# Decays and learning rates per 512 tokens, as short tiles beside the projection tiles

## The chip, the cores and the metric

The kernel runs on one core of one Trainium2 chip. The metric is the time of one execution on the device, in microseconds (us). Times are given as the median of several executions. The profile and the rows below come from one execution that the hardware profiler recorded.

## What is computed

The reference is one layer of a decoder trunk over 2048 tokens of 1024 features, in float32. A mixer sub-layer normalises the input, projects it (`h @ w_in`, 3344 columns) and hands the columns to two groups of heads: gated linear attention (GLA) and an RWKV-7 group, whose outputs go through `w_out`. A gated MLP with a causal convolution follows, the channel mixer. The change touches one part of the RWKV-7 group, where `p` is the token-shifted projection and `c0 : c1 : c2` bound two slices of 64 columns:

```python
w_log = -softplus(-(w0 + tanh(p[..., c0:c1]) @ w_up)) - 0.5
decay = exp(-exp(w_log))                        # per token and channel, 512 channels
a = sigmoid(a0 + p[..., c1:c2] @ a_up)          # the learning rate, 512 channels
k = k * (1 + (a - 1) * k_a)
```

So for each token two small products, each with 64 inputs and 512 outputs, give the logarithm of the decay, the learning rate `a`, and the factor by which `k` is multiplied.

## The kernel before

The 2048 tokens are cut into 4 blocks of 512. Features lie on the 128 partitions, tokens along the free dimension. For each block `stage_b` runs the input projection, one tile of 128 columns after the other: `gemm3` makes 24 matmuls of 128x512 into one PSUM bank (`gbank`, a ring of two banks), three for each of 8 parts of the input, because weight and activation are each split into a high and a low float32r part and three of the four products are kept. `evacuate` then reads the bank: for the RWKV tiles ScalarE scales it (L335), VectorE adds the shifted token (L336), GpSimd mends the first column (L337) and ScalarE keeps the last column for the next block (L338); the result goes to a DRAM tile (`pd`, L339). `ev`, the buffer of the result, is a ring of three.

Weights of the projection are loaded by `Weights`: in block 0 a part is loaded, cast by ScalarE (L190), its low part made by VectorE or GpSimd (L193), and both parts are stored to DRAM as `kept` (L200). Later blocks load the kept parts (L179) into the same two rings of six (`whi`, `wlo`); a projection tile takes two buffers of each.

The recurrences run on units of 128 tokens, 16 in all, 4 per block. `rwkv_p` prepares a unit: it loads its slice of the projections (L776 to L780), turns the values, and makes the decays and rates. That last part is what the change takes out: the tile `wa` holds 64 rows for the decay and 64 for the rate; ScalarE takes the tanh of the first (L792), TensorE makes 4 matmuls for each (L797, L798, plain float32, 64 rows of contraction, 128 tokens) into two banks `rp`, ScalarE takes a tanh of each quarter (L800, L803), GpSimd scales and shifts the results (L801, L805), and VectorE makes the factor of `k` (L804). Then a scan sums the logarithms of the decay (L808), and the rest of the unit follows.

The generator `stage_b` of the next block is the filler of the units: `fill()` is called at several places of a unit and takes, on average, 0.85 tiles each. Block 0's projections run before the units start, beside the first GLA chunks. While the last block's units run, the filler is `spare`, the output projection of the blocks already done. Nothing of the order on the engines is written out by hand: a planner orders all instructions by their priority and by a simulated timeline, gives each tile a free buffer of its ring, and places the waits. All loads are issued from SyncE's queue (SP), stores from SP or from ScalarE's queue.

The channel mixer runs after the units, with its own pools; the change does not touch it.

Of the kernel before, what the change touches and what calls it, by code (L numbers as in the profile page):

```python
# [9 lines left out]
F32 = mybir.dt.float32  # L10
F32R = mybir.dt.float32r
BF16 = mybir.dt.bfloat16
U32 = mybir.dt.uint32
AF = mybir.ActivationFunctionType
ALU = mybir.AluOpType

P = 128
D = 1024
KT = 8
NB = 512  # L20
# [75 lines left out]
def hybrid_kernel(ctx, tc, x, cst, vec, c_row, ada_t, w_in, w_v, w_first, w_z, gk_up, wa_up, g_up,  # L96
# [31 lines left out]
    def vcol(name, k=0, n=1):  # L128
        o, w = _VL[name]
        return vt[:, o + k:o + k + n]  # L130
# [8 lines left out]
    groups = ((TQ, 2), (TK, 2), (TV, 4), (TG, 4), (TZ, 1), (TR, 4), (TRK, 4), (TRV, 4), (TWA, 1), (TPG, 1))  # L139
    pd = [{t0: dram.tile([P, n, NB], F32, name=f"proj_{b}_{t0}") for t0, n in groups} for b in range(NBLK)]  # L140
    mixd = [dram.tile([P, 8, NB], F32, name=f"mix_{b}") for b in range(NBLK)]
# [185 lines left out]

    def evacuate(b, t, ps):
        ev = ap.tile([P, NB], F32, name="ev", tag="ev", bufs=pools["nev"])
        if t < TZ:  # L330
            A.activation(out=ev, in_=ps, func=AF.Copy, scale=0.125 if t < TK else 1.0)
        else:

            m = t - TR
            A.activation(out=ev, in_=ps, func=AF.Copy, scale=omu[:, m:m + 1])  # L335
            V.scalar_tensor_tensor(out=ev[:, 1:NB], in0=ps[:, 0:NB - 1], scalar=vcol("mu", m), in1=ev[:, 1:NB], op0=ALU.mult, op1=ALU.add)  # L336
            G.tensor_tensor(out=ev[:, 0:1], in0=ev[:, 0:1], in1=carry[:, m:m + 1], op=ALU.add)  # L337
            A.activation(out=carry[:, m:m + 1], in_=ps[:, NB - 1:NB], func=AF.Copy, scale=vcol("mu", m))  # L338
        (A if t < TZ else nc.sync).dma_start(out=dst_of(b, t), in_=ev)  # L339
# [23 lines left out]
    def stage_b(b):  # L363

        h = ahead.pop(b)[1]
        order = ([TZ] + list(range(8, TZ)) if b == 0 else list(range(8)) + [TZ] + list(range(8, TZ))) + [TWA, TPG] + [TR + i for i in range(12)]
        for i_, t in enumerate(order):
# [40 lines left out]
            evacuate(b, t, ps)  # L408
# [184 lines left out]
    wa_up = cst1([P, 512], "wa_up", wa_up)  # L593
# [13 lines left out]
    kah = cst1([P, 8], "kah")  # L607
# [162 lines left out]
    def rwkv_p(b, q, n):  # L770
# [3 lines left out]
        wa = ctile([P, CQ], F32, name="rw_wa", tag="rw_wa", bufs=1)  # L774
        pg = ctile([P, CQ], F32, name="rw_pg", tag="rw_pg", bufs=2)
        nc.sync.dma_start(out=wa, in_=pd[b][TWA][:, 0, cs])  # L776
# [15 lines left out]
        A.activation(out=wa[0:64], in_=wa[0:64], func=AF.Tanh)  # L792
        psw, psa = bank("rp"), bank("rp")
        pw_ = psw.rearrange("p (j t) -> p j t", j=4)
        pv = psa.rearrange("p (j t) -> p j t", j=4)
        for j in range(4):
            PE.matmul(out=pw_[:, j, :], lhsT=wa_up[0:64, j * P:(j + 1) * P], rhs=wa[0:64, :], start=True, stop=True)  # L797
            PE.matmul(out=pv[:, j, :], lhsT=wa_up[64:128, j * P:(j + 1) * P], rhs=wa[64:128, :], start=True, stop=True)  # L798
        for j in range(4):
            A.activation(out=lw[:, j], in_=pw_[:, j], func=AF.Tanh, scale=0.5, bias=w0h[:, j:j + 1])  # L800
        G.tensor_scalar(out=lw, in0=lw, scalar1=-0.5 * DECAY, scalar2=-0.5 * DECAY, op0=ALU.mult, op1=ALU.add)  # L801
        for j in range(4):
            A.activation(out=an[:, j], in_=pv[:, j], func=AF.Tanh, scale=0.5, bias=a0h[:, j:j + 1])  # L803
            V.tensor_scalar(out=kp_[:, j], in0=an[:, j], scalar1=kah[:, j:j + 1], scalar2=kah[:, 4 + j:5 + j], op0=ALU.mult, op1=ALU.add)  # L804
        G.tensor_scalar(out=an, in0=an, scalar1=-0.5, scalar2=-0.5, op0=ALU.mult, op1=ALU.add)  # L805
# [695 lines left out]
def layout(inputs):  # L1501
# [26 lines left out]
    for n in ("w0", "a0", "k_k", "k_a", "gn_g", "gn_b"):  # L1528
# [22 lines left out]
        "wa_up": np.concatenate([f("w_lora_up")[0], f("a_lora_up")[0]], 0),  # L1551
# [19 lines left out]
```

## Time and profile before

| | us |
|---|---|
| median of 3 executions | 2924.12 |
| lowest, highest | 2917.79, 2926.74 |
| the profiled execution, its own time | 2920.91 |
| its span (first to last instruction) | 2918.8 |
| TensorE busy in the span | 2746.2 (94%) |
| VectorE busy | 2080.9 (71%) |
| ScalarE busy | 1303.1 (45%) |
| GpSimd busy | 1083.5 (37%) |
| mean granted clock of TensorE | 0.963 |

In the rows below PE is TensorE's matmuls, PEld its weight loads, DVE is VectorE, ACT ScalarE, POOL GpSimd and SP SyncE; a q behind the name is the engine's queue, which issues DMAs. L797 is line 797 of the kernel. `A<-B,C` names the tile written and the tiles read, without buffer numbers. Matmuls overlap: the time from one start to the next is what one takes from the engine, and its own duration is longer. A float32 matmul is recorded as two.

### The profile page before, as it was taken

The numbers are of one execution on the slowest core, as the hardware profiler recorded it, in microseconds if no ns is written. First come the engines' busy times: TensorE is split into PE (matmuls) and PEld (weight loads), VectorE is DVE, ScalarE is ACT, GpSimd is POOL, SyncE is SP. The second block draws the span as 40 slices with busy tenths as digits, with TensorE's granted clock in tenths as the row PEclk, the third lists the DMA queues.
The fourth block names the chain that finished last, engine by engine and source line by source line (L and its number), as shares of the span: only waits on it lengthen the run. The fifth ranks groups of instructions, "written<-read, shape, count | busy, mean of one in ns | idle before, by whom it ended". The sixth has DMA issues, their size and how long they took to land.

```text
span 2918.8 us, 54644 instructions
## 1 busy us (share of the span) xinstructions
PE 2746.2 (94%) x20296; PEld 2224.0 (76%) x20296; DVE 2080.9 (71%) x4103; ACT 1303.1 (45%) x2721; POOL 1083.5 (37%) x1150
## 2 busy tenths in 40 slices
PE   6989999999999999899679999999997999999998
PEld 5777877877787777777567888888776788888887
DVE  7356877757766668876687595775868786685867
ACT  4454435445544455453344352443534444353443
POOL 5223212312122223332456354453436454363541
PEclk9999989999999998999889999999998999999999
DMA  8988955545555565655314424334564633425243
GB/s 285 342 292 305 311 159 175 162 138 164 177 165 145 167 192 189 185 164 168 122 54 152 156 76 159 101 117 149 183 225 140 215 94 128 141 87 162 90 130 110
DMA packets 363530, 486.90 MB, mean 167 GB/s; under 512 B 80768, under 2 KB 153728, under 8 KB 363264
## 3 DMA queue, kind: packets, MB, share of 16 engines
q1 hardware_dynamic: 327984, 447.75, 48.3%
q10 hardware_dynamic: 35280, 35.66, 3.6%
q8 instruction: 160, 2.62, 0.4%
q14 instruction: 106, 0.87, 0.1%
HBM read 342.77 MB, written 140.51 MB: 166 GB/s over the span
## 4 chain that ended last, share of the span: by engine, by line
PE 58%; DVE 10%; DMA 6%; issue 2%; ACT 2%; POOL 2%; SPq 0%; DVEq 0%; ACTq 0%; POOLq 0%
PE g_bank L1270 9%; PE g_bank L1268 9%; PE g_bank L1269 9%; PE g_bank L1325 5%; PE g_bank L1327 5%; PE g_bank L1326 5%; PE g_bank L281 3%; PE g_bank L282 3%; PE g_bank L283 3%; DVE rw_pr L901 1%; DMA rw_k<-proj 1%; DMA acc<-acc 1%; PE gl_bank L698 1%; DMA rw_ln<-inv_a 1%; POOL w_lo L1144 1%
## 5 line engine op out<-in xcount | busy, mean ns | idle before, releaser
L1268 PE MATMUL g_bank<-h_hi,w_hi 128*128 128x512 f32 x1232 | 486.9, 396 | 28.1 <-ACT h_hi L1143 17.2
L1269 PE MATMUL g_bank<-h_lo,w_hi 128*128 128x512 f32 x1232 | 485.8, 394 | 7.7 <-DVE h_lo L1144 4.3
L1270 PE MATMUL g_bank<-h_hi,w_lo 128*128 128x512 f32 x1232 | 478.9, 394 | 7.1 <-POOL w_lo L1144 7.0
L1143 ACT CAST w_hi<-w_st 128x512 fp32r<-128x512 f32 (+1 forms) x396 | 239.0, 608 | 487.0 <-PE g_bank L1326 336.6
L1328 DVE SCALAR_TENSOR_TENSOR acc<-g_bank,mod,acc 128x512 f32<-128x512 f32 (+1 forms) x200 | 144.8, 728 | 248.4 <-PE g_bank L1327 231.7
L281 PE MATMUL g_bank<-h_hi,w_hi 128*128 128x512 f32 x736 | 298.4, 406 | 7.6 <-DMA w_hi<-khi 5.7
L1144 POOL TENSOR_TENSOR w_lo<-w_st,w_hi 128x512 fp32r<-128x512 f32 x154 | 216.7, 1407 | 236.8 <-ACT w_hi L1143 226.0
L1268 PEld LDWEIGHTS g_bank<-h_hi,w_hi 128*128 128x128 f32 x1232 | 234.8, 191 | 82.4 <-ACT h_hi L1143 20.0
L282 PE MATMUL g_bank<-h_lo,w_hi 128*128 128x512 f32 x736 | 293.4, 399 | 0.0
L283 PE MATMUL g_bank<-h_hi,w_lo 128*128 128x512 f32 x736 | 293.3, 399 | 0.1
L1270 PEld LDWEIGHTS g_bank<-h_hi,w_lo 128*128 128x128 f32 x1232 | 234.0, 190 | 61.0 <-POOL w_lo L1144 12.4
L1269 PEld LDWEIGHTS g_bank<-h_lo,w_hi 128*128 128x128 f32 x1232 | 234.2, 190 | 58.8 <-DVE h_lo L1144 5.4
L1325 PE MATMUL g_bank<-hh,w_hi 128*128 128x512 f32 x640 | 251.1, 395 | 5.9 <-DVE acc L1328 5.8
L1326 PE MATMUL g_bank<-hl,w_hi 128*128 128x512 f32 x640 | 251.2, 395 | 0.0
L1327 PE MATMUL g_bank<-hh,w_lo 128*128 128x512 f32 x640 | 251.1, 394 | 0.0
L1144 DVE TENSOR_TENSOR w_lo<-w_st,w_hi 128x512 fp32r<-128x512 f32 (+1 forms) x242 | 201.4, 832 | 18.0 <-ACT w_hi L1143 12.3
L281 PEld LDWEIGHTS g_bank<-h_hi,w_hi 128*128 128x128 f32 x736 | 139.5, 190 | 41.4 <-DMA w_hi<-khi 3.0
L283 PEld LDWEIGHTS g_bank<-h_hi,w_lo 128*128 128x128 f32 x736 | 139.3, 189 | 30.7 <-DMA w_lo<-klo 0.8
L282 PEld LDWEIGHTS g_bank<-h_lo,w_hi 128*128 128x128 f32 x736 | 139.8, 190 | 27.4
L1325 PEld LDWEIGHTS g_bank<-hh,w_hi 128*128 128x128 f32 x640 | 119.8, 187 | 37.0 <-DVE acc L1328 7.1
L1327 PEld LDWEIGHTS g_bank<-hh,w_lo 128*128 128x128 f32 x640 | 119.8, 187 | 29.6
L1326 PEld LDWEIGHTS g_bank<-hl,w_hi 128*128 128x128 f32 x640 | 119.7, 187 | 29.1
(341 smaller groups left out, 6103.4 us busy)
## 6 DMA issues: line engine op xcount, KB each, us to landing
acc<-acc SPq DMA_DIRECT2D x352, 256.0 KB, 3.1
w_hi<-khi SPq DMA_DIRECT2D x188, 256.0 KB, 3.4
w_lo<-klo SPq DMA_DIRECT2D x188, 256.0 KB, 3.8
w_st<-in_ffn_up SPq DMA_DIRECT2D x176, 256.0 KB, 3.0
w_st<-in_ffn_down SPq DMA_DIRECT2D x80, 256.0 KB, 2.7
khi<-w_hi ACTq DMA_DIRECT2D x68, 256.0 KB, 4.1
klo<-w_lo SPq DMA_DIRECT2D x68, 256.0 KB, 4.1
w_st<-in_ada_t SPq DMA_DIRECT2D x64, 256.0 KB, 4.7
```

The lines of the kernel that those rows point to most:

```text
L281: PE.matmul(out=ps, lhsT=wh, rhs=hi, start=k == 0, stop=False)
L282: PE.matmul(out=ps, lhsT=wh, rhs=lo, start=False, stop=False)
L283: PE.matmul(out=ps, lhsT=wl, rhs=hi, start=False, stop=k == KT - 1)
L1143: A.copy(out=hi, in_=t)
L1144: eng.tensor_tensor(out=lo, in0=t, in1=hi.bitcast(F32), op=ALU.subtract)
L1268: PE.matmul(out=ps, lhsT=wh[:, c], rhs=hi, start=first and k == 0, stop=False, skip_group_check=True)
L1269: PE.matmul(out=ps, lhsT=wh[:, c], rhs=lo, start=False, stop=False, skip_group_check=True)
L1270: PE.matmul(out=ps, lhsT=wl[:, c], rhs=hi, start=False, stop=last and k == 3, skip_group_check=True)
L1325: PE.matmul(out=ps, lhsT=wh, rhs=hh, start=j == 0, stop=False)
L1326: PE.matmul(out=ps, lhsT=wh, rhs=hl, start=False, stop=False)
L1327: PE.matmul(out=ps, lhsT=wl, rhs=hh, start=False, stop=j == n - 1)
L1328: V.scalar_tensor_tensor(out=a_, in0=ps, scalar=mod[:, 40 + ft:41 + ft], in1=a_, op0=ALU.mult, op1=ALU.add)
```

## The change

The decays and rates of a block are made once for its 512 tokens, and not for each unit of 128. When the projection tile with the 64 + 64 small inputs (`TWA`) is evacuated, it is no longer stored; `lora` splits it: for each of the two halves a tile of 128 rows holds its high part on 64 rows and its low part on the other 64. The weights are stacked twice along the rows on the host, split once at the start by `Weights`, and kept in DRAM. One matmul with the high weights and one with the low weights then give all four products. There are 8 short tiles a block (4 quarters of 512 channels, for decay and rate), one taken with each of the next 8 projection tiles, each with its own `gbank` bank and its own load of two kept parts of 128x128. Results go to three DRAM tiles `lod`; a unit loads its slices of them.

```diff
-    groups = (... (TRV, 4), (TWA, 1), (TPG, 1))
+    groups = (... (TRV, 4), (TPG, 1))
+    lod = [[dram.tile([P, 4, NB], F32, name=f"lora_{b}_{i}") for i in range(3)] for b in range(NBLK)]
...
+    def lora(b, ev):
+        r0, r1 = slice(0, 64), slice(64, 128)
+        A.activation(out=ev[r0], in_=ev[r0], func=AF.Tanh)
+        both = []
+        for i, (hi, lo) in enumerate(((r0, r1), (r1, r0))):
+            s_ = ap.tile([P, NB], F32R, name=f"lo_s{i}", tag=f"lo_s{i}", bufs=1)
+            A.copy(out=s_[hi], in_=ev[hi])
+            V.tensor_tensor(out=ev[hi], in0=ev[hi], in1=s_[hi].bitcast(F32), op=ALU.subtract)
+            A.copy(out=s_[lo], in_=ev[hi])
+            both.append(s_)
+        yield
+        for i in range(2):
+            for j in range(4):
+                ps = gbank()
+                for p_, s_ in enumerate(("hi", "lo")):
+                    w = pools["w"].tile([P, NB], F32R, name="w_" + s_, tag="w" + s_, bufs=pools["nhl"])[:, 0:P]
+                    nc.sync.dma_start(out=w.bitcast(F32), in_=kept[("lora", i), 0][p_][:, j * P:(j + 1) * P])
+                    PE.matmul(out=ps, lhsT=w, rhs=both[i], start=p_ == 0, stop=p_ == 1)
+                o_ = ap.tile([P, NB], F32, name="ev", tag="ev", bufs=pools["nev"])
+                A.activation(out=o_, in_=ps, func=AF.Tanh, scale=0.5, bias=(w0h, a0h)[i][:, j:j + 1])
+                if i == 1:
+                    k_ = ap.tile([P, NB], F32, name="ev", tag="ev", bufs=pools["nev"])
+                    A.activation(out=k_, in_=o_, func=AF.Identity, scale=kah[:, j:j + 1], bias=kah[:, 4 + j:5 + j])
+                    A.dma_start(out=lod[b][2][:, j, :], in_=k_)
+                A.activation(out=o_, in_=o_, func=AF.Identity, scale=(-0.5 * DECAY, -0.5)[i], bias=kah[:, 8 + i:9 + i])
+                A.dma_start(out=lod[b][i][:, j, :], in_=o_)
+                yield
...
+            if t == TWA:                              # in evacuate, ahead of the store
+                return ev
...
-            evacuate(b, t, ps)                        # in stage_b, after each projection tile
+            ev = evacuate(b, t, ps)
+            if t == TWA:
+                small = lora(b, ev)
+            next(small, None)
             yield
...
-    wa_up = cst1([P, 512], "wa_up", wa_up)
+    for i in range(2):
+        Weights(wa_up[i], cols=NB, key=("lora", i))
...
-        wa = ctile([P, CQ], F32, name="rw_wa", tag="rw_wa", bufs=1)      # in rwkv_p
-        nc.sync.dma_start(out=wa, in_=pd[b][TWA][:, 0, cs])
...
-        A.activation(out=wa[0:64], in_=wa[0:64], func=AF.Tanh)
-        psw, psa = bank("rp"), bank("rp")
-        pw_ = psw.rearrange("p (j t) -> p j t", j=4)
-        pv = psa.rearrange("p (j t) -> p j t", j=4)
-        for j in range(4):
-            PE.matmul(out=pw_[:, j, :], lhsT=wa_up[0:64, j * P:(j + 1) * P], rhs=wa[0:64, :], start=True, stop=True)
-            PE.matmul(out=pv[:, j, :], lhsT=wa_up[64:128, j * P:(j + 1) * P], rhs=wa[64:128, :], start=True, stop=True)
-        for j in range(4):
-            A.activation(out=lw[:, j], in_=pw_[:, j], func=AF.Tanh, scale=0.5, bias=w0h[:, j:j + 1])
-        G.tensor_scalar(out=lw, in0=lw, scalar1=-0.5 * DECAY, scalar2=-0.5 * DECAY, op0=ALU.mult, op1=ALU.add)
-        for j in range(4):
-            A.activation(out=an[:, j], in_=pv[:, j], func=AF.Tanh, scale=0.5, bias=a0h[:, j:j + 1])
-            V.tensor_scalar(out=kp_[:, j], in0=an[:, j], scalar1=kah[:, j:j + 1], scalar2=kah[:, 4 + j:5 + j], op0=ALU.mult, op1=ALU.add)
-        G.tensor_scalar(out=an, in0=an, scalar1=-0.5, scalar2=-0.5, op0=ALU.mult, op1=ALU.add)
+        for t_, from_ in zip((lw, an, kp_), lod[b]):
+            nc.sync.dma_start(out=t_, in_=from_[:, :, cs])
...
-        "wa_up": np.concatenate([f("w_lora_up")[0], f("a_lora_up")[0]], 0),
+        "wa_up": np.stack([np.concatenate([f(n)[0]] * 2, 0) for n in ("w_lora_up", "a_lora_up")]),
```

## Rows read from the trace of the kernel before

**Rows 1.** The page's first part: busy time of each engine in the span.
```profile
PE 2746.2 (94%) x20296; PEld 2224.0 (76%) x20296; DVE 2080.9 (71%) x4103; ACT 1303.1 (45%) x2721; POOL 1083.5 (37%) x1150
```

**Rows 2.** Windows: stretch, length, busy us by engine, granted clock, DMA share, GB/s.
```profile
core 0: us, PE busy (x) PEld busy (x) DVE busy (x) ACT busy (x) POOL busy (x), PEclk, DMA share, GB/s
73.00:115.00 42.00, 41.68 (x199) 31.80 (x198) 10.09 (x14) 19.39 (x35) 6.64 (x6) 1.00 1.02 374
115.00:235.00 120.00, 109.06 (x742) 87.99 (x741) 71.74 (x192) 62.38 (x148) 31.17 (x48) 0.95 0.88 294
235.00:1300.00 1065.00, 1017.85 (x11733) 825.04 (x11734) 763.87 (x2225) 499.93 (x1300) 280.35 (x383) 0.96 0.60 185
1489.00:2918.00 1429.00, 1382.85 (x6080) 1127.23 (x6078) 1048.95 (x1328) 609.90 (x1023) 651.07 (x608) 0.98 0.42 136
```

**Rows 3.** Single tiles and lines: durations (ns min/median/max), first and last start.
```profile
L797 PE MATMUL rp_bank<-rw_wa,wa_up x128: 272/272/579, 237.9 to 1287.7; 64*128 64x128 f32 x128
L798 PE MATMUL rp_bank<-rw_wa,wa_up x128: 272/272/373, 246.2 to 1294.8; 64*128 64x128 f32 x128
...
L335 ACT ACTIVATE ev<-g_bank,omu x56: 664/688/705, 112.3 to 1089.7; 128x512 f32<-128x512 f32 x56
...
L1268 PE MATMUL g_bank<-h_hi,w_hi x1232: 387/389/796, 1420.2 to 2860.7; 128*128 128x512 f32 x176
```

**Rows 4.** Groups by line and form, 235 to 1300 us: busy us, mean ns | idle before, releasers.
```profile
L797 PE MATMUL rp_bank<-rw_wa,wa_up 64*128 64x128 f32 x128 | 22.9, 309 | 0.0
L798 PE MATMUL rp_bank<-rw_wa,wa_up 64*128 64x128 f32 x128 | 20.6, 291 | 0.0
L804 DVE TENSOR_SCALAR rw_kp<-rw_an,kah 128x128 f32<-128x128 f32 x64 | 19.2, 342 | 6.8 <-ACT rw_an L803 6.6
L803 ACT ACTIVATE rw_an<-rp_bank,a0h 128x128 f32<-128x128 f32 x64 | 18.3, 371 | 15.3 <-PE rp_bank L798 14.8 <-PE gl_bank L642 0.4
L800 ACT ACTIVATE rw_lw<-rp_bank,w0h 128x128 f32<-128x128 f32 x64 | 18.3, 369 | 23.7 <-PE rp_bank L797 23.5
L805 POOL TENSOR_SCALAR rw_an<-rw_an 128x512 f32<-128x512 f32 x16 | 15.1, 942 | 18.2 <-DVE rw_kp L804 15.2 <-DVE hn_rk L814 2.3
L801 POOL TENSOR_SCALAR rw_lw<-rw_lw 128x512 f32<-128x512 f32 x16 | 10.0, 623 | 97.2 <-ACT rw_lw L800 97.0
L792 ACT ACTIVATE rw_wa<-rw_wa 64x128 f32<-64x128 f32 x15 | 4.7, 311 | 14.5 <-DMA rw_wa<-proj 14.1
```

**Rows 5.** Timeline of PE around removed groups, one whole, two cut up: start, length.
```profile
245.61 0.39 PE L283 MATMUL g_bank<-h_hi,w_lo 128*128 128x512 f32 x1
245.83 0.39 PE L281 MATMUL g_bank<-h_hi,w_hi 128*128 128x512 f32 x1
246.15 1.16 PE L798 MATMUL rp_bank<-rw_wa,wa_up 64*128 64x128 f32 x8
247.24 0.44 PE L757 MATMUL rp_bank<-ct,rw_kk 128*32 128x8 f32 x32
...
637.08 0.49 PE L283 MATMUL g_bank<-h_hi,w_lo 128*128 128x512 f32 x1
637.51 0.48 PE L797 MATMUL rp_bank<-rw_wa,wa_up 64*128 64x128 f32 x2
637.92 0.50 PE L281 MATMUL g_bank<-h_hi,w_hi 128*128 128x512 f32 x1
```

**Rows 6.** Groups by line and form over the whole span.
```profile
L281 PE MATMUL g_bank<-h_hi,w_hi 128*128 128x512 f32 x736 | 298.4, 406 | 7.6 <-DMA w_hi<-khi 5.7 <-DVE rn L243 1.5 <-ACT ev L331 0.3
L283 PE MATMUL g_bank<-h_hi,w_lo 128*128 128x512 f32 x736 | 293.3, 399 | 0.1
...
L438 DVE TENSOR_TENSOR h_lo<-mx,h_hi 128x512 fp32r<-128x512 f32 x32 | 22.1, 705 | 8.4 <-ACT h_hi L437 8.2
L331 ACT ACTIVATE ev<-g_bank 128x512 f32<-128x512 f32 x28 | 16.6, 596 | 21.5 <-PE g_bank L283 14.6 <-DMA w_st<-in_w_in 3.8 <-DMA khi<-w_hi 1.5
L1192 ACT ACTIVATE ub<-ub,mod 128x512 f32<-128x512 f32 x16 | 11.4, 723 | 15.1 <-DVE ub L1191 14.9
```

**Rows 7.** Timeline at the end of one projection tile of block 0.
```profile
146.68 0.40 PE L283 MATMUL g_bank<-h_hi,w_lo 128*128 128x512 f32 x1
...
147.41 0.68 ACT L335 ACTIVATE ev<-g_bank,omu 128x512 f32<-128x512 f32 x1
...
148.19 0.75 DVE L336 SCALAR_TENSOR_TENSOR ev<-g_bank,vt,ev 128x511 f32<-128x511 f32 x1 [2.68 <-ACT ev L335]
...
149.11 0.26 ACT L338 ACTIVATE carry<-g_bank,vt 128x1 f32<-128x1 f32 x1 [1.02 <-POOL ev L337]
```

**Rows 8.** Timeline of PE where the norm's matmuls (L237, L250) visit a projection bank.
```profile
121.88 0.95 PE L237 MATMUL g_bank<-ones,x_ss 128*128 128x1 f32 x8
...
124.99 0.50 PE L281 MATMUL g_bank<-h_hi,w_hi 128*128 128x512 f32 x1 [1.36 <-DVE rn L243]
...
156.35 0.50 PE L281 MATMUL g_bank<-h_hi,w_hi 128*128 128x512 f32 x1
...
680.34 0.95 PE L663 MATMUL gl_bank<-wlev,gl_gh 128*128 128x384 f32 x4
681.45 0.50 PE L281 MATMUL g_bank<-h_hi,w_hi 128*128 128x512 f32 x1 [0.16 <-DVE rn L243]
...
728.12 0.69 PE L991 MATMUL rs_bank<-rw_sv,rw_t 128*64 128x64 f32 x16
728.73 0.50 PE L281 MATMUL g_bank<-h_hi,w_hi 128*128 128x512 f32 x1
```

**Rows 9.** DMA issues: queue, count, KB each, median us from issue to landing.
```profile
w_lo<-klo SPq DMA_DIRECT2D x188, 256.0 KB, 3.8
...
proj<-ev ACTq DMA_DIRECT2D x44, 256.0 KB, 4.0
```

**Rows 10.** Waits of the SP queue, 235 to 1300 us: total us, times, longest.
```profile
SPq L778 <- DVE rw_rr L872: 18.8, 7, 4.5
SPq L776 <- PE rp_bank L798: 18.6, 10, 6.2
...
SPq L778 <- DVE rw_t L835: 11.9, 3, 8.3
...
SPq L778 <- DVE rw_bk L841: 6.4, 1, 6.4
```

**Rows 11.** Waits of PE, 235 to 1300 us, the longest in total.
```profile
PE rj_bank L924 <- DVE rw_x L918: 7.0, 4, 3.7
```

More of the change, by code (lines that the diff above doesn't have):

```diff
@@ L138, in hybrid_kernel @@
     proj = [[None] * NPROJ for _ in range(NBLK)]
-    groups = ((TQ, 2), (TK, 2), (TV, 4), (TG, 4), (TZ, 1), (TR, 4), (TRK, 4), (TRV, 4), (TWA, 1), (TPG, 1))
+    groups = ((TQ, 2), (TK, 2), (TV, 4), (TG, 4), (TZ, 1), (TR, 4), (TRK, 4), (TRV, 4), (TPG, 1))
     pd = [{t0: dram.tile([P, n, NB], F32, name=f"proj_{b}_{t0}") for t0, n in groups} for b in range(NBLK)]
+    lod = [[dram.tile([P, 4, NB], F32, name=f"lora_{b}_{i}") for i in range(3)] for b in range(NBLK)]
     mixd = [dram.tile([P, 8, NB], F32, name=f"mix_{b}") for b in range(NBLK)]
@@ L365, in stage_b @@
         h = ahead.pop(b)[1]
+        small = iter(())
         order = ([TZ] + list(range(8, TZ)) if b == 0 else list(range(8)) + [TZ] + list(range(8, TZ))) + [TWA, TPG] + [TR + i for i in range(12)]
@@ L606, in hybrid_kernel @@
     V.tensor_scalar(out=a0h, in0=vcol("a0", 0, 4), scalar1=0.5, scalar2=None, op0=ALU.mult)
-    kah = cst1([P, 8], "kah")
+    kah = cst1([P, 10], "kah")
+    V.memset(kah[:, 8:9], -0.5 * DECAY)
+    V.memset(kah[:, 9:10], -0.5)
     V.tensor_scalar(out=kah[:, 0:4], in0=vcol("k_a", 0, 4), scalar1=0.5, scalar2=None, op0=ALU.mult)
```

## The prediction, written before the change was run

> **What bounds the kernel now.** I read the page's totals and slices first, then the stages by window. The matmul engine is busy 94% of the span, every other engine 71% or less [rows 1]. All that the change touches lies ahead of the channel mixer, whose first matmul (L1268) starts at 1420.2 us [rows 3]: the two matmul lines that it removes start between 237.9 and 1294.8 us [rows 3], and what it adds runs beside the projections of blocks 0 to 3, from about 73 us until the last projection is read at 1089.7 us [rows 3]. Two stages differ. From 235 to 1300 us the matmul engine is busy 1017.85 of 1065 us, 95.6%, while DVE is at 72%, ACT at 47%, POOL at 26% and the DMA engines at 0.60 [rows 2]: PE is the bound, and only 47 us of it is idle. From 73 to 235 us, block 0's projections, PE is busy 150.7 of 162 us, but the DMA share is 1.02 and then 0.88 as well [rows 2]: two resources are nearly full there, because weights are loaded, split and stored back for the later blocks. So what the change saves on PE counts in the first of these stages, and what it adds to DMA counts in the second.
>
> **PE work removed.** In 16 units, eight f32 matmuls of 64 rows by 128 columns each, recorded as two passes: 128 records a line. L797 holds PE for 22.9 us and L798 for 20.6 us, 43.5 us together [rows 4]. A group of eight records left whole takes 1.09 us to the next instruction (246.15 to 247.24), so 32 groups would be 34.9 us at the least; where the planner cut it up, one matmul costs 0.41 us, and the split projection matmul before it waits 0.43 us for its successor in place of 0.23 [rows 5]. 43.5 lies between that low end and 32 groups at four such pieces of 0.61 us each (78 us). I keep 43.5. The Trainium skill, TensorEngine Tiling (Array Packing), "When to Use Tiling", would halve it: a contraction of 64 allows two row tiles at once, and L797 and L798 lie on different halves of the rows. By that the saving would be 21.8 us. The rows show groups of one line alone, 1.09 us each, so the rule is not at work here and I don't halve.
>
> **PE work added.** Per block eight short tiles of two split (fp32r) matmuls of 128x512: 64 in all. That shape follows its neighbour every 0.23 us [rows 5], so 14.7 us; by its recorded 399 to 406 ns it would be at most 26 [rows 6]. They have the type of the projection matmuls around them, so no switch of type is paid. 48 of them (11.0 us) run beside units, 16 (3.7 us) in block 0. From 235 us on the net is 11.0 - 43.5 = -32.5 us of PE work. With PE 95.6% busy most of that should come back as time; the units' own chain must follow, so I take 80%, -26 us, with -32.5 and 0 as ends.
>
> **The two projection banks.** All g_bank tiles share two PSUM banks. Now a projection tile fills one while the other is read. A short tile between two projections takes the second bank, so that the next projection needs either the first bank again, released when L335, L336 and L338 are through, or the short tile's, released after one ACT read. In one tile the last matmul starts at 146.68 and L338 ends at 149.37, 2.7 us later; L336 waits behind other DVE work and L338 behind L336 [rows 7]. Minus the short tile's 0.46 us and the usual 0.23 that is 2.0 us a tile. By the short tile's own bank it is less: it waits for L335 (0.69 [rows 3]), then reads 0.60 us (the nearest row, L331 [rows 6]), about 1.2 us. Queued behind the waiting matmul are all recurrence matmuls that the planner put after it. The trace has natural cases: the sum and spread matmuls of the next block's norm visit the same two banks between projections. In block 0 the projection after them waited 1.36 us in one case and not at all in the other; in two cases beside units 0.16 us and nothing, because recurrence matmuls stood in the gap [rows 8]. I take the means: 8 x 0.68 = 5.4 us in block 0, 24 x 0.08 = 1.9 us later. The ends are 0 and 32 x 2.0 = 64 us. The Trainium skill, Perfetto Trace Analysis, "Optimizing Tensor Performance", asks that independent matmul groups rotate through different banks, so that one's evacuation overlaps the next group's matmuls; this change takes that rotation away at 32 places, and full waits at all of them would be the 64 us. The four cases agree with it only in block 0.
>
> **DMA.** Set-up: the stacked weights are 512 KB in place of 256 KB, and their four parts of 256 KB are stored, 1.3 MB more. A block: sixteen weight loads of 64 KB, twelve result stores of 256 KB, less one projection store, 3.9 MB more. A unit: three loads of 256 KB for one of 64 KB, 0.7 MB. From 115 to 235 us 294 GB/s go at a share of 0.88, so 120 us hold about 40 MB at full share; there are 35.3 now and 39.2 afterwards. It just fits, but the stage before is at 1.02 [rows 2], and the set-up's 1.3 MB at its 374 GB/s are 3.5 us. The three ev buffers are also held until such a store lands, 4.0 us [rows 9], and a short tile takes one or two of them per 5.5 us projection. I take 3 us for block 0, with 0 and 18 us (5.2 MB at 294 GB/s) as ends. Later blocks have a share of 0.60 and hide it. Weights share the ring of six hi and six lo parts; a projection takes two of each, a short tile one, so the prefetch falls from three tiles to two, 11 us of matmuls against a landing of 3.8 us [rows 9]: nothing. On SP the loads of a unit's decays and rates wait for the matmuls of the unit before (they share tiles with them), and weight loads queue behind; the nearest waits, the three of L778 for DVE work of the unit before, sum to 37.1 us with a longest of 8.3, while L776's 18.6 us go with its load [rows 10]. The same 11 us of prefetch hides them; bare, they would cost up to 37 us.
>
> **The other engines.** ACT loses L800, L803 and L792, 41.3 us [rows 4], and gains per block some 25 instructions of 512 columns at about 0.65 us (L331 0.60 to L1192 0.72 [rows 6]), 65 us, and 16 us of DMA issues. At 47% it hides this; if it didn't, the 40 us more would be the bill. DVE loses 19.2 us and gains eight half-height subtractions of 0.7 us; POOL loses about 25 us [rows 4, 6]. None is the bound, so nothing is counted; shorter DVE queues can only make L336 earlier.
>
> **Sum.** -26 + 3.7 (short tiles in block 0) + 5.4 + 1.9 + 3 = -12 us. The profiled execution took 2920.91 us (span 2918.8), which gives 2908.9; the median of the runs shown is 2924.12, 3.2 higher, which gives 2912. I predict 2912.
>
> **Rivals.**
> 1. The banks decide (slower). Place: the first projection matmul after each of the 32 short tiles. Price: 1.2 us uncovered each, 38 us, in place of 7.3: 2912 + 31 = 2943. It beats the saving from (26 - 3.7 - 3) / 32 = 0.6 us a tile on. For it: DVE's queue delays L336, a matmul engine that issues in order cannot pass the wait, and stalls can bring half clock (granted 0.95 and 0.96 in these stages [rows 2]). Against it: rows 8, where the planner had other matmuls for the gap. 19%.
> 2. No change. The units' own chain (ACT, DVE, small DMAs between steps) sets the pace, and freed PE time turns into idle PE time; only 10 of the 32.5 us come back: 2924 - 10 + 14 = 2928. For it: the idle PE time between 235 and 1300 us is spread over waits for ACT and DVE inside the recurrence (7.0 us for rw_x alone) [rows 11]. Against it: it is 4.4% in all. 17%.
> 3. More than forecast. The two rp banks that each unit no longer holds, and a shorter chain from projection to decay, let recurrence steps start earlier: all 32.5 us come back, 10 of the 47 us of idle time too, and block 0 takes only the 10 us: 2924 - 42 + 10 = 2892. For it: L800 and L803 waited 38 us for these matmuls, and POOL 97 us for L800 [rows 4]; against it: most of that is idle time of engines that bound nothing. 14%.
>
> **How the numbers follow.** 0.3% of 2924 us is 8.8 us, about what a measurement of this kernel tells from no change: below 2915 is faster, above 2933 slower. The forecast has 50%, of it 38 faster and 12 same (own range 2900 to 2921). Rival 1 gives 16 slower, 2 same, 1 faster; rival 2 gives 14 same, 3 slower; rival 3 gives 14 faster. Faster 53%, same 28%, slower 19%. The planner orders everything anew, and the bank waits (0 to 64 us) and the DMA term (0 to 18) are open, so the range goes to both outer rivals: 2886 to 2943.
>
> **What would show it.** Right: PE busy from 235 us to the end of the mixer falls by some 30 us at about the same idle time, and the first L1268 moves from 1420.2 us to about 1408; block 0's end moves later by about 12 us. Wrong: first projection matmuls with idle time before them, ended by carry or by the short tile's Tanh, of over 0.6 us each (rival 1); the same end of the mixer with more idle PE time (rival 2); or a DMA share near 1 and idle PE in block 0 beyond 12 us. If the stage from 1489 us on [rows 2] changes its length by more than 5 us, something outside this sum has moved.

## The result, and the profile after

The changed kernel takes 2964.45 us (median of 4 executions, 2961.08 to 2972.63) against 2922.22 for the kernel before: ratio 1.0155, 95% interval 1.0137 to 1.0174. It is 42 us slower; 2912 was predicted, and the range ended at 2943. The profiled execution took 2961.08 us, 40.2 more than that of before.

The page's first part, to set beside [rows 1]:

```profile
PE 2762.7 (93%) x20104; PEld 2224.7 (75%) x20104; DVE 2068.7 (70%) x4051; ACT 1326.8 (45%) x2679; POOL 1063.0 (36%) x1118
```

There are 192 PE records fewer (256 went, 64 came), and yet 16.5 us more of PE time. The lines have new numbers: L281 and L283 are now L283 and L285, L331 is L362, L335 to L338 are L366 to L369, L1268 is L1294. First the lines that answer to [rows 3]: the short tiles' matmuls and their Tanh, the projection's evacuation, and the first matmul of the channel mixer.

```profile
L348 PE MATMUL g_bank<-lo_s,w_hi x32: 387/393/499, 121.6 to 1097.6; 128*128 128x512 f32 x32
...
L348 PE MATMUL g_bank<-lo_s,w_lo x32: 387/394/505, 121.9 to 1097.8; 128*128 128x512 f32 x32
...
L350 ACT ACTIVATE ev<-g_bank,w0h x16: 676/684/702, 123.4 to 1055.5; 128x512 f32<-128x512 f32 x16
...
L366 ACT ACTIVATE ev<-g_bank,omu x56: 670/688/696, 113.8 to 1146.7; 128x512 f32<-128x512 f32 x56
...
L1294 PE MATMUL g_bank<-h_hi,w_hi x1232: 387/389/796, 1461.9 to 2901.4; 128*128 128x512 f32 x176
```

The first channel mixer matmul was to move from 1420.2 us to 1408; it moved to 1461.9. So all 42 us are lost ahead of it. I cut what is ahead where block 0's last projection tile is read: at 212.3 us before, at 233.8 after. Windows by stage (columns as in [rows 2]), first before, then after:

```profile
115.00:212.30 97.30, 88.84 (x618) 72.47 (x617) 54.22 (x152) 49.23 (x123) 24.05 (x39) 0.98 0.89 296
212.30:1420.20 1207.90, 1147.37 (x13016) 928.99 (x13016) 849.16 (x2447) 557.67 (x1431) 327.06 (x432) 0.95 0.60 185
1420.20:2918.00 1497.80, 1420.25 (x6276) 1153.09 (x6276) 1109.29 (x1407) 641.75 (x1078) 688.14 (x638) 0.97 0.41 132
```

```profile
115.00:233.80 118.80, 105.19 (x655) 83.96 (x654) 58.09 (x152) 67.56 (x156) 24.91 (x40) 0.93 0.84 283
233.80:1461.90 1228.10, 1150.57 (x12851) 921.72 (x12849) 833.24 (x2398) 563.78 (x1360) 295.16 (x396) 0.94 0.65 202
1461.90:2959.00 1497.10, 1420.01 (x6230) 1151.97 (x6228) 1111.16 (x1402) 641.30 (x1076) 697.77 (x641) 0.97 0.41 132
```

Two losses of like size: block 0 is 21.5 us longer (12.1 predicted), blocks 1 to 3 are 20.2 us longer (24.1 shorter predicted). The channel mixer stays within 0.7 us. In blocks 1 to 3 PE's busy time should have fallen by 32.5 us to 1114.9; it is 1150.57, 35.7 us dearer than that, and idle PE time grew from 60.5 to 77.5 us. The same stretches, instructions on the tiles g_bank (first line) and rp_bank (second) alone; the first busy time is PE's. Before, then after:

```profile
212.30:1420.20 1207.90, 665.55 (x2904) 491.90 (x2904) 50.95 (x73) 65.58 (x129) 0.95 0.60 185
212.30:1420.20 1207.90, 163.72 (x1568) 125.42 (x1568) 102.32 (x256) 78.48 (x224) 0.95 0.60 185
```

```profile
233.80:1461.90 1228.10, 704.54 (x2953) 511.15 (x2953) 50.14 (x72) 80.20 (x152) 0.94 0.65 202
233.80:1461.90 1228.10, 137.30 (x1312) 105.40 (x1312) 102.30 (x256) 42.08 (x96) 0.94 0.65 202
```

The ring rp lost the 256 records of the small products, 43.5 us [rows 4], but only 26.4 us of time: the 1312 matmuls that stayed went from 120.2 to 137.3 us. The ring g gained 49 records and 39.0 us, where 48 short matmuls at 0.23 are 11 us. Work that the change doesn't touch became dearer on PE. The groups of the projection matmuls over the whole span, beside 406 and 399 ns in [rows 6], show it too:

```profile
L283 PE MATMUL g_bank<-h_hi,w_hi 128*128 128x512 f32 x736 | 307.2, 418 | 21.4 <-ACT ev L350 13.4 <-DMA w_hi<-khi 6.0 <-ACT carry L369 1.4
...
L285 PE MATMUL g_bank<-h_hi,w_lo 128*128 128x512 f32 x736 | 301.0, 409 | 0.0
...
L834 DVE TENSOR_TENSOR_SCAN rw_lw<-ct,rw_lw 128x256 f32<-128x256 f32 x32 | 20.9, 687 | 18.9 <-DMA rw_lw<-lora 18.9
...
L850 DVE TENSOR_TENSOR rw_kp<-rw_kp,rw_k 128x512 f32<-128x512 f32 x16 | 11.1, 693 | 21.1 <-DMA rw_k<-proj 20.9
```

How a matmul gets dearer is seen best in block 0, where one of the bank waits stands open (timeline; start, length; the answer to [rows 7, 8]). PE alone, then what ACT did in its gap:

```profile
165.57 0.40 PE L348 MATMUL g_bank<-lo_s,w_hi 128*128 128x512 f32 x1
165.80 0.40 PE L348 MATMUL g_bank<-lo_s,w_lo 128*128 128x512 f32 x1
170.51 0.80 PE L283 MATMUL g_bank<-h_hi,w_hi 128*128 128x512 f32 x1 [4.32 <-ACT ev L350]
171.11 0.63 PE L284 MATMUL g_bank<-h_lo,w_hi 128*128 128x512 f32 x1
171.54 0.63 PE L285 MATMUL g_bank<-h_hi,w_lo 128*128 128x512 f32 x1
...
173.67 0.40 PE L284 MATMUL g_bank<-h_lo,w_hi 128*128 128x512 f32 x1
173.91 0.39 PE L285 MATMUL g_bank<-h_hi,w_lo 128*128 128x512 f32 x1
```

```profile
166.18 1.28 ACT L686 ACT_TABLE_LOAD   x1
...
167.47 0.42 ACT L686 ACTIVATE gl_ga<-gl_ga 128x256 f32<-128x256 f32 x1
...
167.79 0.67 ACT L366 ACTIVATE ev<-g_bank,omu 128x512 f32<-128x512 f32 x1
...
168.48 1.28 ACT L350 ACT_TABLE_LOAD   x1
...
169.78 0.69 ACT L350 ACTIVATE ev<-g_bank,a0h 128x512 f32<-128x512 f32 x1
```

The next projection's first matmul waits for the short tile's Tanh (L350), and that stands in ACT's queue behind a GLA exponential, the projection's own evacuation and two table loads of 1.28 us. PE idles 4.32 us. Then it issues at every 0.43 us in place of 0.23. The windows of that time show why (the column before the DMA share is the granted clock):

```profile
164.00:166.00 2.00, 2.00 (x11) 1.50 (x9) 0.75 (x1) 1.26 (x3) 0.00 (x0) 1.00 0.76 264
...
168.00:170.00 2.00, 0.00 (x0) 0.00 (x0) 1.60 (x4) 1.97 (x3) 0.19 (x1) 1.00 0.99 300
170.00:172.00 2.00, 1.49 (x4) 1.20 (x5) 0.42 (x1) 1.75 (x5) 0.00 (x0) 0.57 1.08 382
172.00:174.00 2.00, 2.00 (x7) 1.57 (x6) 0.00 (x0) 0.59 (x1) 0.00 (x0) 0.58 0.92 340
174.00:176.00 2.00, 2.00 (x11) 1.65 (x10) 0.56 (x1) 0.62 (x1) 0.00 (x0) 1.00 0.66 182
```

After the wait the granted clock is near its lower level (1.2 GHz) for about 3 us (170.51 to 173.67), and the dense matmuls that resume run in it: the wait is paid a second time, in part, by work that did not wait.

### The profile page after: what moved, and what is told of

Read it like the earlier page. It is cut to its first block, busy times and chain, and to the rows that moved or that the text cites. A ratio compares the mean times of both kernels' runs of the same rounds, so it can differ in the third digit from the quotient of the medians.

```text
span 2959.3 us, 54526 instructions
## 1 busy us (share of the span) xinstructions
PE 2762.7 (93%) x20104; PEld 2224.7 (75%) x20104; DVE 2068.7 (70%) x4051; ACT 1326.8 (45%) x2679; POOL 1063.0 (36%) x1118
## 4 chain that ended last, share of the span: by engine, by line
PE 65%; DVE 14%; DMA 10%; ACT 4%; issue 2%; POOL 1%; SPq 1%; ACTq 0%; DVEq 0%; POOLq 0%
PE g_bank L1296 9%; PE g_bank L1294 9%; PE g_bank L1295 8%; PE g_bank L1351 5%; PE g_bank L1353 5%; PE g_bank L1352 5%; PE g_bank L283 4%; PE g_bank L284 3%; PE g_bank L285 3%; DVE rw_pr L927 1%; DMA rw_lw<-lora 1%; PE gl_bank L738 1%; PE g_bank L487 1%; PE g_bank L489 1%; PE g_bank L488 1%
## 5 line engine op out<-in xcount | busy, mean ns | idle before, releaser
L1294 PE MATMUL g_bank<-h_hi,w_hi 128*128 128x512 f32 x1232 | 486.7, 395 | 26.2 <-ACT h_hi L1169 13.8
L1295 PE MATMUL g_bank<-h_lo,w_hi 128*128 128x512 f32 x1232 | 486.2, 395 | 12.7 <-DVE h_lo L1170 8.0
L283 PE MATMUL g_bank<-h_hi,w_hi 128*128 128x512 f32 x736 | 307.2, 418 | 21.4 <-ACT ev L350 13.4
L1170 POOL TENSOR_TENSOR w_lo<-w_st,w_hi 128x512 fp32r<-128x512 f32 x154 | 222.9, 1448 | 232.9 <-ACT w_hi L1169 222.1
L284 PE MATMUL g_bank<-h_lo,w_hi 128*128 128x512 f32 x736 | 301.6, 410 | 0.0
L285 PE MATMUL g_bank<-h_hi,w_lo 128*128 128x512 f32 x736 | 301.0, 409 | 0.0
L1294 PEld LDWEIGHTS g_bank<-h_hi,w_hi 128*128 128x128 f32 x1232 | 234.4, 190 | 81.5 <-ACT h_hi L1169 17.1
L283 PEld LDWEIGHTS g_bank<-h_hi,w_hi 128*128 128x128 f32 x736 | 144.4, 196 | 58.1 <-ACT ev L350 15.2
L285 PEld LDWEIGHTS g_bank<-h_hi,w_lo 128*128 128x128 f32 x736 | 144.0, 196 | 32.1 <-DMA w_lo<-klo 0.6
L1351 PEld LDWEIGHTS g_bank<-hh,w_hi 128*128 128x128 f32 x640 | 119.8, 187 | 35.7 <-DVE acc L1354 5.2
```

Source lines behind the costliest of these rows:

```text
L283: PE.matmul(out=ps, lhsT=wh, rhs=hi, start=k == 0, stop=False)
L284: PE.matmul(out=ps, lhsT=wh, rhs=lo, start=False, stop=False)
L285: PE.matmul(out=ps, lhsT=wl, rhs=hi, start=False, stop=k == KT - 1)
L1170: eng.tensor_tensor(out=lo, in0=t, in1=hi.bitcast(F32), op=ALU.subtract)
L1294: PE.matmul(out=ps, lhsT=wh[:, c], rhs=hi, start=first and k == 0, stop=False, skip_group_check=True)
L1295: PE.matmul(out=ps, lhsT=wh[:, c], rhs=lo, start=False, stop=False, skip_group_check=True)
```

## The experiments

Each time is a median, with its ratio to the kernel before and the 95% interval. The theories: B, the projection banks (rival 1). C, the unit's new loads. D, the block's splits, evacuations, stores and weight loads. H, what is lost is TensorE work beside the chain's waits. P, the order that the planner writes anew. W, the change's parts simply add up.

**Another bank for the short tiles (e1_rp).**

```diff
-                ps = gbank()
+                ps = bank("rp")        # in lora
```

> The changed kernel (2964) with one edit: the short tiles take their banks from the ring rp, which the units no longer use for these products, and not from the two projection banks. Theory B (projection tiles wait for a bank, 21 us of idle PE time before them, and the half clock that follows these waits): 2964 - 21 - about 20 = 2923, and the waits of L283 and L487 for L350 gone. Theory D (DMA, ev buffers, weight ring) and theory C (late loads of decays and rates into the units): 2955 to 2970, no change. Theory P (the planner's new order alone): anything within 15 of 2964.

2973.99 us, 1.0177 (1.015 to 1.0205). Not cured. But block 0's last projection tile is read at 215.9 us in place of 233.8, so there the banks are most of the loss (17.9 of 21.5 us); blocks 1 to 3 take 1243.0 us in place of 1228.1. Units use ring rp too, but that this is the reason is not shown: e13_rp0 below leaves the ring to them there and takes longer still.

**The kernel before without the small products (e2_nomm)**; decays and rates are left out.

```diff
-        psw, psa = bank("rp"), bank("rp")
-        (the eight matmuls of L797, L798)
+        pw_ = pv = VV
```

> The kernel before with the small matmuls L797 and L798 and their two banks left out; the two tanh read the values tile instead, so decays and rates are not those of the reference and all else stays. It measures what the removal is worth by itself. If PE bounds the units: 43.5 us at 80 to 100% come back, 2922 - 35 to 43 = 2879 to 2887. If the units' own chain sets the pace: 2912 or more.

2912.53 us, 0.9966 (0.9944 to 0.9987). This is the whole saving with none of its price: 43.5 us of PE work taken out give 10 us (4 to 16), in this one order of the instructions. The stage of blocks 1 to 3, and in it g_bank and rp_bank:

```profile
209.50:1407.30 1197.80, 1118.40 (x12738) 900.62 (x12736) 852.78 (x2452) 557.79 (x1425) 334.46 (x431) 0.94 0.61 188
...
209.50:1407.30 1197.80, 677.82 (x2898) 500.74 (x2896) 50.41 (x72) 65.71 (x128) 0.94 0.61 188
209.50:1407.30 1197.80, 125.33 (x1312) 94.04 (x1312) 102.50 (x256) 41.99 (x96) 0.94 0.61 188
```

PE's busy time falls by 29.0 us, idle time grows from 60.5 to 79.4, and the projection matmuls cost 12 us more than before. So of the 43.5 us, 10.1 shorten the stage, 18.9 turned into waiting, and 14.5 went into matmuls that became dearer, at a granted clock of 0.94 in place of 0.95.

**The changed kernel without the short tiles' matmuls, banks and weight loads (e4_nops)**; the results are made from the split operand instead.

```diff
-                ps = gbank()
-                (for "hi", "lo": load the kept part, matmul)
+                ps = both[i].bitcast(F32)
```

> The changed kernel with the short tiles' matmuls, banks and weight loads left out; their tanh reads the split operands instead, so decays and rates are not the reference's. The split, all ACT work, the ev buffers, the result stores and the units' loads stay. Theory B or the weight ring: the whole loss goes and the saving shows, 2922 - 35 = 2887 to 2900. Theory D in its other part (stores, ev buffers) or theory C (loads into the units): 2940 or more.

2942.26 us, 1.007 (1.0047 to 1.0092). About half of the loss goes; 30 us above e2_nomm stay, with no short matmul left.

**A small shift of the order (e6_lag).** The kernel before, lag 366 for 370 (the priority by which the filler's instructions stand behind the unit's).

> The kernel before with the filler's priority lag 366 in place of 370: no work changes, only the planner's order. Theory P: it moves by 10 us or more either way (2905 or less, 2932 or more). Otherwise 2915 to 2930.

2922.31 us, 1.0009 (0.9991 to 1.0027): a shift of 4 does nothing.

**The unit's side alone (e11_loads).** The kernel before, with the three loads, from tiles of constants, in place of small products and tanh.

```diff
-        (L792 to L805: tanh, small products, scale, shift)
+        for t_, from_ in zip((lw, an, kp_), lod):
+            nc.sync.dma_start(out=t_, in_=from_[:, :, cs])
```

> The kernel before with the unit side of the change alone: no load of rw_wa, no small products, no tanh, scale or shift of lw, an and kp_ in the unit; in their place the three loads of 256 KB, from tiles that hold constants (written once, beside block 0's TWA tile). It leaves the decays and rates out, so their values are constants. The kernel without the small products alone (e2_nomm) took 2912.5 us. Theory C (the three loads put a wait into the unit chain, on rw_lw, rw_an and rw_kp, and the unit chain sets the pace): the saved tanh and DVE operations are lost again and more, 2925 to 2940 us, and the trace shows DVE's scan of rw_lw waiting on its DMA some 1 us or more in most of the 32 units. Theory D (the loss is on the block's side: splits, banks, evictions, stores, weight loads): the loads cost nothing and the unit is shorter than in e2_nomm, 2895 to 2912 us.

2931.43 us, 1.0036 (1.002 to 1.0052), in the range of theory C: 19 us above e2_nomm, though ACT, DVE and POOL have less to do. But 13 of the 32 scans wait for `rw_lw`, where theory C had most of them. DVE's waits from 114 to 1420 us (us, times, longest):

```profile
...
DVE rw_kp L817 <- DMA rw_k<-proj: 23.9, 11, 3.8
...
DVE rw_lw L801 <- DMA rw_lw<-lora: 19.3, 13, 4.5
```

**The block's side alone (e9_both).** The kernel before with its small products, plus the short tiles in full; no unit loads their results.

> The kernel before as it is, plus the block side of the change in full: the split operands, eight short tiles beside the projection tiles, their banks, weight loads, evictions and stores; nobody loads the results. It measures what the block side costs by itself. By the sum of the prediction it is 14.7 us of matmuls x 80%, 3.7 + 5.4 + 1.9 + 3 us, so 2948 us. Theory D (block side takes all the loss, loads are free): about 2964 - 2900 + 2922, so 2975 to 2990 us. Theory C (the loads take half of it): 2945 to 2962 us. In block 0 alone, where no unit runs, the trace should show the projections ending near 234 us, as after the change, under either theory.

2983.59 us, 1.021 (1.0174 to 1.0246): 62 us for what the prediction's terms put at 23 (the 26 of the expectation counts the short tiles of block 0 twice). 17.3 us of them are in block 0 (last tile read at 229.6), 44.5 in blocks 1 to 3. But the same addition to e11_loads costs 33 us only (2931.43 to 2964.45). So the price of a part depends on what it is added to.

**Two buffers for the decays (e12_two).** The changed kernel; the next unit's load of `rw_lw` need not wait for the operand that takes the decays' place.

```diff
-        lw, an, kp_ = qp("rw_lw"), qp("rw_an"), qp("rw_kp")
+        lw, an, kp_ = qp("rw_lw", bufs=2), qp("rw_an"), qp("rw_kp")
```

> The changed kernel with two buffers for rw_lw (the decays of a unit and the r operand that later takes their place no longer wait for one another), so that the load of the next unit's decays can be issued a recurrence earlier. Theory C: the wait of the scan on the load of rw_lw (18.9 us in 11 waits after the change) goes, and the time falls by 8 to 20 us, to 2945 to 2956 us; by how much shows whether the waits on loads are on the path. Theory D: the wait goes and the time stays within 5 us of 2964, because the vector engine then waits for rw_k's load or for the matmuls instead.

2989.9 us, 1.0243 (1.0206 to 1.0279). Neither theory, and no test of the two: the wait that was to go stayed, 18.9 us in 11 waits after the change and here

```profile
...
DVE rw_lw L834 <- DMA rw_lw<-lora: 22.4, 10, 4.1
```

What makes this run 25 us slower is not shown; the planner's order changed with the buffer.

**Another lag after the change (e10_lag300).**

> The changed kernel with the planner's lag at 300 in place of 370: the units and the block's work are woven in another order, everything else as after the change (2964.5 us). Theory P (the loss is chance in the order that the planner writes, such as where the short tiles fall among the recurrence's matmuls): it moves by more than 10 us, either way. Theories C and D: within 8 us of 2964, that is 2956 to 2972 us.

2982.43 us, 1.0221 (1.0179 to 1.0264): 18 us more by the order alone. Theory P had to be taken seriously.

**Ring rp in block 0 alone (e13_rp0).**

```diff
-                ps = gbank()
+                ps = gbank() if b else bank("rp")        # in lora
```

> The changed kernel with the short tiles' banks taken from ring rp in block 0 alone, where hardly a unit runs, and from the projections' own banks in blocks 1 to 3. With ring rp everywhere (e1_rp) the projections of block 0 ended at 215.9 us in place of 233.8, but blocks 1 to 3 took 1243 us to the first FFN matmul in place of 1228. Theory B (in block 0 the short tiles' banks are the loss, 18 us): projections of block 0 end near 216 us and the whole takes 2944 to 2952 us. Theory D (the block's splits, evictions and stores are late whatever the bank) or P (any shift of the order costs as much later as it gives): 2958 us or more.

2971.66 us, 1.0164 (1.0132 to 1.0195). Block 0 and blocks 1 to 3 in windows:

```profile
115.00:217.30 102.30, 97.68 (x649) 79.62 (x648) 57.31 (x150) 65.87 (x153) 24.85 (x41) 0.98 0.97 330
217.30:1472.20 1254.90, 1170.88 (x12888) 930.04 (x12886) 839.36 (x2405) 567.32 (x1367) 292.52 (x396) 0.93 0.64 198
```

Block 0 gives back 16.5 us, its clock is 0.98 again, and blocks 1 to 3 take 26.8 us more, with the same code.

**No products and no loads (e14_memset).** As e11_loads, but GpSimd sets the three tiles to constants.

```diff
+        for t_, c_ in zip((lw, an, kp_), (-0.3, -0.5, 0.5)):
+            G.memset(t_, c_)
```

> The kernel before without the small products and their tanh, scale and shift, and without any load in their place: GpSimd sets lw, an and kp_ to constants in every unit (decays and rates are left out). The same with three loads (e11_loads) took 2931.4 us, the same with the tanh kept on other data (e2_nomm) 2912.5 us. Theory C (the loads themselves are late and hold the unit chain): about 20 us below e11_loads, 2900 to 2915 us. Theory H (what is lost is TensorE work that stood beside the chain's waits, so that the recurrence and projection matmuls behind it run at the half clock): the same loss without a load, 2922 to 2935 us.

2918.68 us, 0.9988 (0.9974 to 1.0001), between the two ranges. With the loads it is 12.7 us more, without any of the work 2.7 us less than before. Of the 18.9 us from e2_nomm to e11_loads, 12.7 go with the loads, as theory C has it, and 6.2 stay without them, as theory H has it. Taking all of L792 to L805 out is worth next to nothing, which speaks for theory H. DVE's wait for `rw_k` is there without any new load:

```profile
...
DVE rw_kp L810 <- DMA rw_k<-proj: 20.7, 11, 4.5
```

**The lag of the kernel before (b_lag300).**

> The kernel before with the planner's lag at 300 in place of 370. After the change the same step cost 18 us. Theory P (the order before is a favourable one, and any larger shift of it costs 10 to 20 us, the change among them): 2932 to 2945 us. If the order matters only after the change: within 6 us of 2921.

2967.88 us, 1.0165 (1.014 to 1.0191): 46 us from one constant, with not one operation changed. Then the same at more lags, for both kernels (b_ is before, a_ and e10_ after).

**Lag 440 after (e10_lag440).**

> The changed kernel with the planner's lag at 440. Theory P: it moves by more than 8 us from 2964.5, and if it falls, part of the loss was the lag that no longer fits. If the loss lies in the added work and waits themselves: 2958 to 2972 us.

2963.84 us, 1.0148 (1.0124 to 1.0171), the same as at lag 370.

**Lag 340 before (b_lag340).**

> The kernel before with lag 340. Theory P (370 is a narrow favourable point, almost any other order loses): above 2935 us. Theory W (the loss at 300 is a real limit of too short a lag; the change's loss is its own work and waits): 2918 to 2930 us here.

2916.57 us, 0.9985 (0.9966 to 1.0004). Blocks 1 to 3 at lag 300, and in them g_bank and rp_bank; then the same at 340:

```profile
216.10:1461.20 1245.10, 1191.04 (x13096) 959.15 (x13096) 847.73 (x2453) 557.22 (x1433) 316.81 (x428) 0.93 0.58 179
...
216.10:1461.20 1245.10, 692.16 (x2904) 499.54 (x2904) 51.19 (x73) 65.29 (x129) 0.93 0.58 179
216.10:1461.20 1245.10, 182.49 (x1568) 141.37 (x1568) 103.06 (x256) 78.41 (x224) 0.93 0.58 179
```

```profile
214.20:1409.70 1195.50, 1129.71 (x13016) 915.07 (x13016) 845.48 (x2447) 554.30 (x1430) 321.47 (x428) 0.96 0.61 187
...
214.20:1409.70 1195.50, 665.06 (x2904) 493.30 (x2904) 50.92 (x73) 65.55 (x129) 0.96 0.61 187
214.20:1409.70 1195.50, 158.28 (x1568) 122.87 (x1568) 102.57 (x256) 78.41 (x224) 0.96 0.61 187
```

The same work costs PE 1191.0 us in one order and 1129.7 in the other, at less idle time in the dearer one (54.1 against 65.8 us): the order sets the price of a matmul. The granted clock (0.93 against 0.96) would make 1129.7 us into 1166, an estimate, so some 36 of the 61 us go with it; that the rest comes from what stands next to a matmul is not shown.

**Lag 340 after (a_lag340).**

> The changed kernel with lag 340. Theory P: within 15 us of the kernel before at lag 340, since both then have an order that nobody chose. Theory W: 30 to 45 us above the kernel before at lag 340, 2955 to 2975 us.

2971.92 us, 1.0171 (1.0139 to 1.0204): 55 us above the kernel before at the same lag, a larger distance than either theory had; the time itself lies in theory W's range.

**Lag 440 before (b_lag440).**

> The kernel before with lag 440; the changed kernel took 2963.8 us there. Theory P: 2935 to 2965 us. Theory W: 2918 to 2930 us, which leaves the change 35 to 45 us dearer at equal lag.

2942.76 us, 1.0066 (1.0046 to 1.0086): 21 us below the changed kernel.

**Lag 400 after (a_lag400).**

> The changed kernel with lag 400. Theory P: one of the lags tried falls clearly below 2950 us or this one moves by more than 8 us from 2964. Theory W: 2958 to 2970 us, as at 370 and 440.

2946.98 us, 1.0083 (1.0053 to 1.0112): 17 us below lag 370, as theory P had it.

**Lag 400 before (b_lag400).**

> The kernel before with lag 400. Theory W: 2915 to 2930 us, so the change costs 20 to 32 us at this lag. Theory P: anything from 2915 to 2950 us, with no steady distance from the changed kernel (the distances so far: 15 us at lag 300, 55 at 340, 42 at 370, 21 at 440).

2928.5 us, 1.002 (1.0 to 1.0041), inside both ranges.

**Both remedies (e13_400).** Lag 400, and ring rp in block 0.

> The changed kernel with lag 400 and, in block 0, the short tiles' banks from ring rp: block 0's projections end some 18 us earlier. Theory W (the parts of the change add up): 2929 to 2936 us, against 2947 with lag 400 alone. Theory P (what block 0 gains is lost again in the order of blocks 1 to 3, as at lag 370, where 16.5 us earlier in block 0 gave nothing): 2943 us or more.

2944.22 us, 1.0073 (1.0049 to 1.0096). The median is not to be told from that of lag 400 alone. In the two traces, a_lag400 first, block 0 ends 20 us earlier, blocks 1 to 3 take 1211.0 us in both, and so the channel mixer starts 20 us earlier:

```profile
237.90:1448.90 1211.00, 1137.61 (x12883) 913.36 (x12881) 829.51 (x2398) 562.32 (x1362) 290.12 (x396) 0.95 0.67 205
```

```profile
217.80:1428.80 1211.00, 1135.73 (x12776) 903.11 (x12775) 827.75 (x2397) 564.38 (x1359) 295.81 (x397) 0.95 0.66 205
```

But the profiled execution of e13_400 was the shortest of its eight (2935.03) and that of a_lag400 the longest of its four (2952.01); by the medians 3 us of the 20 are left. Whether the gain in block 0 is lost again later is open at this lag.

Together, in us. The times are medians; the end of block 0 and the length of blocks 1 to 3 come from one trace each, and executions of one of these kernels differ by up to 23 us:

| lag | before: time | block 0 ends | blocks 1-3 | after: time | block 0 ends | blocks 1-3 | after - before |
|---|---|---|---|---|---|---|---|
| 300 | 2967.9 | 216.1 | 1245.1 | 2982.4 | 235.3 | 1237.6 | 14.5 |
| 340 | 2916.6 | 214.2 | 1195.5 | 2971.9 | 234.9 | 1227.5 | 55.3 |
| 370 | 2922.2 | 212.3 | 1207.9 | 2964.5 | 233.8 | 1228.1 | 42.3 |
| 400 | 2928.5 | 211.6 | 1210.8 | 2947.0 | 237.9 | 1211.0 | 18.5 |
| 440 | 2942.8 | 212.7 | 1226.0 | 2963.8 | 234.1 | 1229.0 | 21.0 |
| mean | 2935.6 | 213.4 | 1217.1 | 2965.9 | 235.2 | 1226.6 | 30.3 |

At every lag the change is slower, by 30 us in the mean and by 30 between the best of each. Of the mean, 22 us arise in block 0 at every lag alike (19 to 26), and about 10 in blocks 1 to 3, where the distance swings from -7.5 to 32 us with the order. No version of the change tried here beats the kernel before.

## Why the prediction was wrong

**The saving (80% of 32.5 us, -26 us): the step that failed.** The removal of 43.5 us was real, but that PE's 95.6% would bring most of it back was not: e2_nomm has the removal alone and gains 10 us. The prediction took busy time as a fixed sum of work. It isn't: with the products gone PE waits longer (idle 60.5 to 79.4 us) and the matmuls that stay cost 14.5 us more. That the products had stood in the gaps of the unit chain fits this, and is not shown. It is rival 2's mechanism, which I gave 17%; that its 10 us, then of 32.5, came out as well is luck, and its 2928 us was 36 too low. One run could owe 10 us to its order, but blocks 1 to 3, forecast 24.1 us shorter, are 9.6 us longer in the mean of the five lags and at best 7.5 shorter. So this stage misses its forecast by 33.7 us in the mean, and block 0 by 9.7. Split the other way, the unit's side alone (e11_loads) costs 10 us where the sum had it save 34.8 (80% of 43.5), and the rest of the change 33 us where the sum had 23, each in one order.

**The banks in block 0 (0.68 us a tile, 5.4 us): too small.** Other banks in block 0 give 16.5 us back (e13_rp0), 2.1 us for each of the 8 tiles in the mean. That this is near the end of 2.0 from [rows 7] is chance: that end was a wait for L338, and PE waits here for the short tile's own read, L350. By the windows 9.0 of the 16.5 us are idle PE time (13.6 against 4.6), 1.1 a tile, and 7.5 dearer matmuls at a granted clock of 0.93 against 0.98. The idle part is near the 1.2 us that the prediction gave this wait, though in four long waits and not in eight; by its own rows that is 0.69 + 0.60 = 1.29. I took the mean of two cases from [rows 8], where only small matmuls of the norm visit the bank. The DMA share fell to 0.84, and e13_rp0 moves the same at 0.97 in less time, so DMA did not bind; with the short tiles' 3.7 us, 1.3 of e13_rp0's 5.0 us remain for the 3 I had given DMA. PE's waits in block 0 after the change (us, times, longest), and then that in blocks 1 to 3:

```profile
PE g_bank L283 <- ACT ev L350: 8.9, 4, 4.3
...
PE g_bank L239 <- ACT ev L350: 1.2, 1, 1.2
```

```profile
...
PE g_bank L283 <- ACT ev L350: 4.5, 3, 2.5
```

The Trainium skill, Perfetto Trace Analysis, "Optimizing Tensor Performance", wants independent matmul groups to rotate through different banks. The run with other banks agrees in block 0, by 16.5 us. Rival 1 did not hold beyond: in blocks 1 to 3 the same wait sums to 4.5 us in 3 cases, for 1.9 predicted. I had the short tile read 0.60 us right behind L335, and forgot what else ACT has queued there: GLA's exponentials with their table loads.

**The loads, at nothing.** From e14_memset to e11_loads the three loads add 12.7 us, which can also be the order. DVE now waits 18.9 us for the load of `rw_lw`, where before it waited 3.2 us for GpSimd's result, so the claimed cover of 11 us did not reach DVE there. The 20.9 us for `rw_k` are not the new loads': e14_memset has 20.7 without any. Whether these waits are on the path is open, since e12_two, which was to take one away, did not. ACT's additions (65 us by estimate) came as said: ACT is busy 23.7 us more, which is 65 less the 41.3 removed. No run here gives them a price of their own.

**The planner's order, named in one sentence and given no size.** It is the largest effect seen in blocks 1 to 3: lags from 300 to 440 move the kernel before by 51 us and the changed one by 35. Of the 42 us at lag 370, about 12 lie above the mean distance of 30, and by the order alone they could as well lie below.

Of the signs that the prediction named, two were seen: the channel mixer did not move (0.7 us), and block 0 shows waits over 0.6 us ended by the short tile's Tanh. PE's busy time in blocks 1 to 3 grew by 3.2 us where it was to fall by some 30. ([rows 5] shows 0.22 us for a dense matmul and not the 0.23 of the sum, which moves its 14.7 us by 0.6.)

What stays open: which of the new neighbours makes which matmul dearer in blocks 1 to 3. As the lag alone moves one kernel by up to 51 us, the difference between two single runs of different code there (the 10 us of e2_nomm and the 12.7 from e14_memset to e11_loads among them) can be the order, and no run here holds the order fixed while a part goes. What is shown is block 0, where other banks give 16.5 us back, and the mean over five lags.

## What to carry to other kernels

Busy time of an engine whose price depends on its neighbours is no budget: take the work out alone first, and see what comes back. Where a planner orders the instructions, measure a change at several settings of the planner, for both kernels, before a part of the change gets the blame. A tile put between two others in a ring of two banks can cost the whole queue of the engine that reads it, not the length of the read.

## What had not been expected of the hardware

One wait of 4.32 us was followed by two windows of 2 us at a granted clock of 0.57 and 0.58, in which the projection matmul took 0.43 us to the next in place of 0.23. Of 13,016 to 13,096 recorded matmuls of the same work, the busy time ran from 1129.7 to 1191.0 us, 5%, when only the planner's lag was changed.
